# FFN chunks with stationary weights and two streaming token tiles in a one-core macaron layer

## The chip, the cores and the metric

The kernel runs on one core of a Trainium2 chip, in one launch. The metric is the device time of that launch in microseconds (us). The core has TensorE (PE; its weight loads are listed apart as PEld), VectorE (DVE), ScalarE (ACT), GpSimd (POOL), SyncE (SP, whose queue issues the weight transfers) and 16 DMA engines. PE multiplies a stationary operand of 128 x 128, which is loaded first, with a moving operand that streams through column by column, and adds into PSUM, here used as eight banks of 128 x 512 fp32.

## The reference

One decoder layer on 256 tokens of width 1024: an FFN, a token mixer, a second FFN, each behind an RMSNorm and a shift and scale that come from a vector c, and each added to h through a gate. The two FFNs are what the change touches:

```python
def swiglu(n, w_gate, w_up, w_down):
    return (jax.nn.silu(n @ w_gate) * (n @ w_up)) @ w_down
...
        sh1, sc1, gt1, sh2, sc2, gt2, sh3, sc3, gt3 = jnp.split(mod, N_MOD, axis=-1)
        n = modulate(rmsnorm(h, g_ffn1[l]), sh1, sc1)
        h = h + 0.5 * gt1 * swiglu(n, w1_gate[l], w1_up[l], w1_down[l])
        n = modulate(rmsnorm(h, g_mix[l]), sh2, sc2)
        h = h + gt2 * hybrid_mixer(n, w_in[l], w_pool[l], pool_scale[l], w_out[l])
        n = modulate(rmsnorm(h, g_ffn2[l]), sh3, sc3)
        h = h + 0.5 * gt3 * swiglu(n, w2_gate[l], w2_up[l], w2_down[l])
    return rmsnorm(h, g_final)
```

The shapes: n is 256 x 1024, w_gate and w_up are 1024 x 2816, w_down is 2816 x 1024, all fp32.

## The kernel before

**Numbers.** Every fp32 matrix is held as two parts, hi (rounded to the type fp32r, which PE takes) and lo (the rest, value minus hi). A product is three matmuls: hi by hi, lo by hi, hi by lo.

**Tiles.** The 256 tokens are two tiles of 128 (t = 0, 1). The width 1024 is eight k-tiles of 128. The 2816 hidden columns are 11 chunks of 256. All weights are read once, as transfers of 1 MB into one of four raw buffers, on SP's queue, in the order of the list that `plan` writes; each is then cast in two halves, hi on ACT (L290) and lo on DVE (L291), into 11 buffers of each kind. Units called "ada" in that list are not cast: DVE reduces them against c (L279) into the shifts, scales and gates, between the casts.

**Lead chunks and rest chunks.** The first chunks of each FFN (0 to 5 of FFN 1, 0 to 3 of FFN 2) are computed k-tile by k-tile while the normalised rows come in; the change leaves them as they are. The rest chunks are 6 to 10 of FFN 1 and 4 to 10 of FFN 2. For one of these, `ffn_chunk` (L399) computes for one token tile the 128 x 512 result "gate columns, then up columns" in one PSUM bank: tokens (128 x 128 of nh or nl) are stationary, and 512 weight columns stream, 8 k-tiles x 3 products = 24 matmuls (L396, L397). `swiglu` (L410) makes pr = Silu(gate) x up, tokens on the partitions: ACT's Silu reads PSUM (L413), DVE multiplies (L416). The second FFN product needs the hidden columns on the partitions, so `hidden_t` (L419) turns pr with two PE transposes per token tile (L422) and splits the turned tile into hh on ACT (L310) and hl on DVE (L311). `down` (L429) then multiplies these, stationary, with the down weights, 512 columns streaming, into accumulators (accf) that stand in four PSUM banks of their own (L437). Where the last two chunks of FFN 2 are added into half-banks, the matmuls are 256 columns wide (L449).

**Order.** `ffn_rest` (L494) runs over the rest chunks. In a turn it computes the chunk for t = 0, turns the chunk before it (L499), computes t = 1, and then runs down for the chunk before it. The last four chunks' down products (HOLD) are kept for the end of the FFN, where they lie under the residual's work. FFN 2's first rest chunk, 4, stands outside that loop (L909 to L913), and there it is the lead chunks 0 and 1 that are turned between the two token tiles. Small drains are marked urgent; the order of each engine's queue is set by a scheduler that goes by priorities and its own estimate of when things are ready. Pools decide which buffer a tile gets: `psp` has four PSUM banks, given out in turn, for chunk results, transposes and gates (`gate_rows`, one PE transpose behind chunk 9 of each FFN); a new tile in a bank waits until the last reader of the old one is done.

**Names in the trace.** gu is a chunk's result, ht a turned tile, le and ld lead chunks, prl their products, raw/hi/lo the weights, nha/nla the tokens of FFN 1 and nhc/nlc those of FFN 2; in a listing of instructions gu1_4_0 is FFN 2, chunk 4, token tile 0.

Of the kernel before, what the change touches and what calls it, by code (L numbers as in the profile page):

```python
# [10 lines left out]
F32 = mybir.dt.float32  # L11
# [161 lines left out]
def block_kernel(ctx, tc, w, vec, x, c, gf, wpool, bandd, biasd, out):  # L173
# [224 lines left out]

    def ffn_chunk(f, ci, n, t, between={}):  # L399
        ps = psp.tile([P, 512], F32, name=f"gu{f}_{ci}_{t}", tag="ps")  # L400
        for hf in range(2):
            hi, lo = want("gu", (f, ci, hf))
            for k in range(4):
                if 4 * hf + k in between:
                    between[4 * hf + k]()
                gemm(ps, n[t][0], n[t][1], 4 * hf + k, cols(hi, k), cols(lo, k),
                     hf == 0 and k == 0, hf == 1 and k == 3)
        return ps

    def swiglu(f, ci, t, ps, pr=None):  # L410
# [17 lines left out]

    def down(f, ci, t, hid, accs, banks=(0, 1)):  # L429
        hi, lo = want("down", (f, ci))  # L430
        hh, hl = hid
        steps = []
        for k in range(2):
            first, last = ci == 0 and k == 0, ci == NCH - 1 and k == 1
            for (a, ww, st, sp) in ((hh, hi, first, False), (hl, hi, False, False), (hh, lo, False, last)):
                for b in banks:
                    steps.append(mm(accs[b], a[:, k, :], cols(ww, 2 * k + b), start=st, stop=sp))  # L437
        return steps

    def down_halves(f, chunks, hid, acc_b, other):  # L440

        for c0, ps in ((0, acc_b), (256, other)):
            n = 0
            for ci in chunks:
                hi, lo = want("down", (f, ci))
                for k in range(2):
                    for a, ww in ((hid[ci][0], hi), (hid[ci][1], hi), (hid[ci][0], lo)):
                        n += 1
                        mm(ps[:, 0:256], a[:, k, :], cols(ww, 2 * k + 1)[:, c0:c0 + 256], start=c0 > 0 and n == 1,  # L449
                           stop=n == 6 * len(chunks))  # L450
# [42 lines left out]

    def ffn_rest(f, ci0, n, prev, pci, accs, finish, gate):  # L494
        hid = {}
        for ci in range(ci0, NCH):
            ps0 = ffn_chunk(f, ci, n, 0)
            pr0 = swiglu(f, ci, 0, ps0)
            hid[pci] = [hidden_t(f, pci, t, prev[t]) for t in range(NT)]  # L499
            ps1 = ffn_chunk(f, ci, n, 1)  # L500
            pr1 = swiglu(f, ci, 1, ps1)
            if pci < NCH - HOLD:
                for t in range(NT):
                    down(f, pci, t, hid[pci][t], accs[t])
            prev, pci = [pr0, pr1], ci
            if ci == NCH - 2:
                gate()
        last = range(NCH - HOLD, NCH)
        for ci in last[:-1]:
            down(f, ci, 0, hid[ci][0], accs[0])  # L510
        hid[NCH - 1] = [hidden_t(f, NCH - 1, t, prev[t]) for t in range(NT)]
        down(f, NCH - 1, 0, hid[NCH - 1][0], accs[0])
        after = finish(0)
        steps = []
        for banks in ((0, 1),) if f == 0 else ((0,), (1,)):
            for ci in last:
                if after and ci == last[TURN]:
                    after(steps)
                if f == 0 or banks == (0,) or ci < SPLIT[0]:
                    steps += down(f, ci, 1, hid[ci][1], accs[1], banks)  # L520
        if f == 1:
# [26 lines left out]
    xs, rs, turned = [], [], []  # L548
    n1 = [new_n(f"a{t}") for t in range(NT)]
    with in_order() as last:  # L550
# [81 lines left out]
    def hids(ci):  # L632
        return [hidden_t(0, ci, t, prs[ci][t]) for t in range(NT)]

    def both_down(ci, hid):
        for t in range(NT):
            down(0, ci, t, hid[t], nm["acc"][t])

# [102 lines left out]
    def heads_out(hp, v, y):  # L741
# [5 lines left out]
        with urgent():  # L747
            for t in range(NT):
                nc.scalar.copy(y[t][0][:, 4 + hp, :], ps[:, ts(t, P)])
            for t in range(NT):  # L750
                nc.vector.tensor_tensor(y[t][1][:, 4 + hp, :], ps[:, ts(t, P)], y[t][0][:, 4 + hp, :].bitcast(F32),
                                        ALU.subtract)

    def pool_group(g, u, y):
# [62 lines left out]
    def wout(t, banks, after=None):  # L817
        steps = []
        for n, i in enumerate(WOUT):
# [87 lines left out]

    prs = lead_out(1, lead, (2, 3, 0, 1))
    ps0 = ffn_chunk(1, LEAD, n3, 0)  # L909
    pr0 = swiglu(1, LEAD, 0, ps0)  # L910
    hid = [[hidden_t(1, ci, t, prs[ci][t]) for t in range(NT)] for ci in range(2)]
    ps1 = ffn_chunk(1, LEAD, n3, 1)
    pr1 = swiglu(1, LEAD, 1, ps1)  # L913
# [34 lines left out]
```

## Time and profile before

| | |
|---|---|
| median of 3 runs | 480.79 us (480.66 to 481.0) |
| the profiled execution | 481.04 us, of which the span (first to last instruction) is 479.2 us |
| granted PE clock, mean | 0.997 of full speed |
| FFN weights and others read | 124.61 MB, 262 GB/s over the span |
| FFN 1's rest chunks and downs | about 109.9 to 187 us |
| FFN 2's chunk 4, first rest chunk | starts near 330 us |

The rest of the page stands in the prediction, where it is used. In rows of groups the columns are line, engine, operation, out<-in, shapes and count, then busy us and mean ns of one, then the engine's idle time just before them and what ended it. In rows of a timeline they are start, duration, engine, line, operation; a row "x4" is four instructions in one.

### The profile page before, as it was taken

To read this page: it belongs to the slowest core of one execution; us is meant where nothing else is said; L and a number is where in the kernel's file an instruction comes from. 1 tells how busy PE (TensorE), PEld (TensorE's weight loads), DVE (VectorE), ACT (ScalarE), POOL (GpSimd) and SP (SyncE) were. 2 spreads that over 40 slices of the span, in tenths; PEclk is the share of its full clock that TensorE was granted. 3 is DMA by queue.
4 is the path that set the end of the run, shared out by engine and by line. 5 is a ranking of instruction groups with operands and counts; after the bars stand their busy time and mean duration, and the time that the engine had idled before them with its cause. 6 is when DMAs were issued, how large, how long until landed. Compare 5 with 4: busy or idle time off the path is not lost.

```text
span 479.2 us, 6028 instructions
## 1 busy us (share of the span) xinstructions
PE 469.0 (98%) x2188; PEld 381.2 (80%) x2188; DVE 355.8 (74%) x577; ACT 260.9 (54%) x447; POOL 13.4 (3%) x35
## 2 busy tenths in 40 slices
PE   8999999999999999999999999999999999999994
PEld 4678888888888888888878888888878888888883
DVE  4988899996987893789999868946666855655244
ACT  3686585454454460896877288845643543444121
POOL 1000000000000000110001000000000000000010
PEclk9999999999999999999999999999999999999998
DMA  8999995998988892579878944985457648630102
GB/s 302 412 349 345 358 347 186 351 420 356 351 316 329 302 379 122 221 279 377 334 284 334 346 177 178 376 324 176 176 180 271 260 191 327 230 122 0 44 1 88
DMA packets 19215, 126.05 MB, mean 263 GB/s; under 512 B 2329, under 2 KB 2865, under 8 KB 4850
## 3 DMA queue, kind: packets, MB, share of 16 engines
q1 hardware_dynamic: 17568, 121.12, 66.5%
q0 software_dynamic: 1184, 3.98, 2.4%
q10 hardware_dynamic: 434, 0.58, 0.3%
q8 instruction: 17, 0.28, 0.2%
q14 instruction: 12, 0.10, 0.1%
HBM read 124.61 MB, written 1.06 MB: 262 GB/s over the span
## 4 chain that ended last, share of the span: by engine, by line
PE 88%; ACT 5%; DMA 3%; issue 1%; DVE 1%; POOL 0%; POOLq 0%; DVEq 0%
PE accf L437 22%; PE gu L396 18%; PE gu L397 9%; PE le L485 9%; PE ld L485 8%; PE accm L829 5%; PE zp L396 4%; DMA raw<-in_w_dram 3%; PE zp L397 2%; PE ht L422 2%; ACT hi L290 2%; PE ld L396 2%; PE sh L396 2%; ACT nhb L367 1%; ACT n32b L368 1%
## 5 line engine op out<-in xcount | busy, mean ns | idle before, releaser
L291 DVE TENSOR_TENSOR lo<-raw,hi 128x1024 fp32r<-128x1024 f32 (+1 forms) x156 | 183.8, 1209 | 41.4 <-ACT hi L290 32.3
L290 ACT CAST hi<-raw 128x1024 fp32r<-128x1024 f32 (+1 forms) x156 | 158.2, 1045 | 74.9 <-DMA raw<-in_w_dram 32.3
L279 DVE CUSTOM_DVE_ANT_0 raw<-raw,cb,vecs 128x1024 f32<-128x1024 f32 x70 | 88.0, 1281 | 2.0 <-DMA raw<-in_w_dram 2.0
L437 PE MATMUL accf<-hi,hh 128*128 128x512 f32 x172 | 54.5, 394 | 0.2
L437 PE MATMUL accf<-hi,hl 128*128 128x512 f32 x172 | 54.2, 391 | 0.0
L437 PE MATMUL accf<-lo,hh 128*128 128x512 f32 x172 | 53.8, 389 | 0.0
L396 PE MATMUL gu<-hi,nhc 128*128 128x512 f32 x112 | 44.4, 396 | 0.0
L413 ACT ACTIVATE sg<-gu 128x256 f32<-128x256 f32 x24 | 9.2, 381 | 64.5 <-PE gu L397 64.5
L397 PE MATMUL gu<-lo,nhc 128*128 128x512 f32 x112 | 43.7, 390 | 0.0
L396 PE MATMUL gu<-hi,nlc 128*128 128x512 f32 x112 | 43.6, 390 | 0.0
L437 PEld LDWEIGHTS accf<-lo,hh 128*128 128x128 f32 x172 | 32.3, 188 | 6.8
L437 PEld LDWEIGHTS accf<-hi,hl 128*128 128x128 f32 x172 | 32.0, 188 | 7.2 <-DVE hl L311 0.7
L437 PEld LDWEIGHTS accf<-hi,hh 128*128 128x128 f32 x172 | 31.7, 188 | 7.2 <-ACT hh L310 1.1
L416 DVE TENSOR_TENSOR pr<-sg,gu 128x256 f32<-128x256 f32 x24 | 10.1, 419 | 33.1 <-ACT sg L413 33.1
L396 PE MATMUL gu<-hi,nha 128*128 128x512 f32 x80 | 31.7, 396 | 0.0
L397 PE MATMUL gu<-lo,nha 128*128 128x512 f32 x80 | 31.2, 390 | 0.0
L396 PE MATMUL gu<-hi,nla 128*128 128x512 f32 x80 | 31.1, 389 | 0.0
L311 DVE TENSOR_TENSOR hl<-ht,hh 128x256 fp32r<-128x256 f32 x44 | 16.5, 418 | 14.4 <-ACT hh L310 14.4
L310 ACT CAST hh<-ht 128x256 fp32r<-128x256 f32 x44 | 14.1, 379 | 23.0 <-PE ht L422 23.0
L396 PE MATMUL zp<-hi,nhb 128*128 128x512 f32 x64 | 26.1, 408 | 0.0
L397 PE MATMUL zp<-lo,nhb 128*128 128x512 f32 x64 | 25.0, 391 | 0.0
L396 PE MATMUL zp<-hi,nlb 128*128 128x512 f32 x64 | 25.0, 390 | 0.0
(193 smaller groups left out, 722.0 us busy)
## 6 DMA issues: line engine op xcount, KB each, us to landing
raw<-in_w_dram SPq DMA_DIRECT2D x112, 1024.0 KB, 5.7
raw<-in_w_dram SPq DMA_DIRECT2D x4, 512.0 KB, 7.8
gt<-gd POOLq DMA_DIRECT2D x3, 512.0 KB, 4.2
h<-in_x_dram SPq DMA_DIRECT2D x2, 512.0 KB, 4.7
bias<-in_bias_dram POOLq DMA_DIRECT2D x2, 512.0 KB, 3.7
band_all<-in_band_dram POOLq DMA_DIRECT2D x1, 544.0 KB, 3.6
gfb<-in_gf_dram POOLq DMA_DIRECT2D x1, 512.0 KB, 5.5
out_dram<-o SPq DMA_DIRECT2D x4, 128.0 KB, 2.5
```

Of the source, the lines that this page charges most:

```text
L279: note(nc.vector.tensor_tensor_reduce(r, r, cb, 1.0, vecs[:, m:m + 1], ALU.mult, ALU.add, mod[:, m:m + 1]), i, 1)
L290: note(nc.scalar.copy(hi[:, o:o + n], src), i + s / 2, 0)
L291: note(nc.vector.tensor_tensor(lo[:, o:o + n], src, hi[:, o:o + n].bitcast(F32), ALU.subtract), i + s / 2, 0)
L310: nc.scalar.copy(hi_ap, src)
L311: nc.vector.tensor_tensor(lo_ap, src, hi_ap.bitcast(F32), ALU.subtract)
L396: return [mm(ps, nh[:, k, :], whi, start=first, stop=False), mm(ps, nl[:, k, :], whi, start=False, stop=False), mm(ps, nh[:, k, :], wlo, s ...
L397: mm(ps, nh[:, k, :], wlo, start=False, stop=last)]
L416: nc.vector.tensor_tensor(pr, sg, ps[:, 256:512], ALU.mult)
L422: nc.tensor.transpose(pt[:, i, :], pr[:, ts(i, P)], ident)
L437: steps.append(mm(accs[b], a[:, k, :], cols(ww, 2 * k + b), start=st, stop=sp))
L485: done.append(mm(banks[ci][t], n[t][a][:, j, :], cols(ww, lead_set(f, j).index(ci)), start=j == 0 and p == 0, stop=last and p == 2))
L829: steps.append(mm(acc2[t][b], a[:, k, :], cols(ww, 2 * kk + b), start=st, stop=sp))
```

## The change

For the rest chunks the two operands change places. `block` computes 128 hidden columns (block b = 0 or 1 of the chunk's 256) for all 256 tokens: the weights are stationary, 128 x 128 at a time, and the tokens stream. The result has hidden columns on the partitions, so it needs no turning. A block fills two PSUM banks, e = 0 for gate and e = 1 for up. For each k-tile and each e there are two matmuls: the hi weights against hi and lo tokens of both tiles, 512 columns wide (hi results in the bank's first 256 columns, lo results in its last 256), and the lo weights against the hi tokens, 256 wide, added to the first 256 columns. When a block is done, ACT copies the last 256 columns of each bank out and DVE adds the first 256 to them; then follow Silu (ACT), the product (DVE) and the split into hh and hl (ACT, DVE), all on 128 x 256.

So that both tiles, hi and lo, can stream from one access, the token tiles lie in one SBUF tile `rounded` (as much memory as before; `homes` says which slot a new token tile takes). An operand of 512 columns is then four stretches of 128 in that tile. For the mixer's output y, tile 1 keeps its k-tiles in the order k ^ 4 (`slot`), the same work in other places. In the weight array, a rest chunk's two units are now cut by block b (all k-tiles of 128 gate and 128 up columns) and not by k-half; sizes and order of the transfers stay. In both FFNs the lead chunks that were turned inside a rest chunk are now turned between its block 0 and its block 1, once in FFN 1 (chunk 3's two token tiles, in chunk 6) and once in FFN 2 (those of chunks 0 and 1, in chunk 4).

The core of the diff:

```diff
+TURNED = (6, 4)
...
+        elif kind == "gu" and a[1] >= TURNED[a[0]]:
+            w[i].reshape(P, KD, 2, P)[:] = gu[a[0]][:, :, a[1], :, P * a[2]:P * a[2] + P].transpose(1, 0, 2, 3)
...
+    rounded = npool.tile([P, 2, 3, KD, P], F32R, name="rounded")
+    homes = iter((0, 1, 2, 1, 2, 0, 0, 1))
+
+    def new_n():
+
+        i = next(homes)
+        return rounded[:, 0, i], rounded[:, 1, i]
...
-    def ffn_chunk(f, ci, n, t, between={}):
-        ps = psp.tile([P, 512], F32, name=f"gu{f}_{ci}_{t}", tag="ps")
-        for hf in range(2):
-            hi, lo = want("gu", (f, ci, hf))
-            for k in range(4):
...
-                gemm(ps, n[t][0], n[t][1], 4 * hf + k, cols(hi, k), cols(lo, k),
-                     hf == 0 and k == 0, hf == 1 and k == 3)
...
+    def block(f, ci, b):
+
+        his, los = want("gu", (f, ci, b))
+        ps = [psp.tile([P, 2 * S], F32, name=f"bl{f}_{ci}_{b}{e}", tag="ps") for e in range(2)]
+        for k in range(KD):
+            for e in range(2):
+                o = slice((k % 4) * 2 * P + e * P, (k % 4) * 2 * P + e * P + P)
+                mm(ps[e].rearrange("p (a t c) -> p a t c", a=2, t=NT), his[k // 4][:, o], rounded[:, :, 0:NT, k, :],
+                   start=k == 0, stop=False)
+                mm(ps[e][:, 0:S].rearrange("p (t c) -> p t c", t=NT), los[k // 4][:, o], rounded[:, 0, 0:NT, k, :],
+                   start=False, stop=k == KD - 1)
...
+        with urgent():
...
+            for dst, src in ((sg, ps[0]), (pr, ps[1])):
+                nc.scalar.copy(dst, src[:, S:2 * S])
+                nc.vector.tensor_tensor(dst, src[:, 0:S], dst, ALU.add)
+            nc.scalar.activation(sg, sg, AF.Silu)
+            nc.vector.tensor_tensor(pr, pr, sg, ALU.mult)
+            split(hh, hl, pr)
+        return hh, hl
+
+    def blocks(f, ci, between={}):
+        both = []
+        for b in range(2):
+            both.append(block(f, ci, b))
+            if b in between:
+                between[b]()
+        return [[[a[:, ts(t, P)] for a in both[k]] for k in range(2)] for t in range(NT)]
...
         for ci in range(ci0, NCH):
-            ps0 = ffn_chunk(f, ci, n, 0)
-            pr0 = swiglu(f, ci, 0, ps0)
-            hid[pci] = [hidden_t(f, pci, t, prev[t]) for t in range(NT)]
-            ps1 = ffn_chunk(f, ci, n, 1)
-            pr1 = swiglu(f, ci, 1, ps1)
+            hid[ci] = blocks(f, ci, {0: turn_prev} if turn_prev else {})
+            turn_prev = None
             if pci < NCH - HOLD:
...
+    hid[LEAD] = blocks(1, LEAD, {0: lambda: hid.update({ci: hidden(1, ci, prs[ci]) for ci in range(2)})})
```

`down` and `down_halves` take their stationary slices from the new layout; they run the same matmuls.

**The order on the engines** at FFN 2's chunk 4. First PE of the kernel before, from the last matmul of token tile 0 to the first of tile 1 (ident is the unit matrix of a transpose, accf100 an accumulator; a number at a name's end only tells tiles apart):

```order
L397 MATMUL gu1_4_0_3097<-lo86_1_2911,nhc0_2683 128x512
L422 MATMUL ht1_0_0_3146<-ident_92,prl11_3072 128x128 x2
L422 MATMUL ht1_0_1_3153<-ident_92,prl11_3072 128x128 x2
L422 MATMUL ht1_1_0_3160<-ident_92,prl11_3072 128x128 x2
L437 MATMUL accf100_3203<-hi87_0_2947,hh1_0_0_3149 128x512
L437 MATMUL accf101_3204<-hi87_0_2947,hh1_0_0_3149 128x512
L422 MATMUL ht1_1_1_3167<-ident_92,prl11_3072 128x128 x2
L396 MATMUL gu1_4_1_3174<-hi85_0_2832,nhc1_2806 128x512
```

The same place on PE after the change, from the end of block 0 to the start of block 1:

```order
L437 MATMUL bl1_4_01_3193<-rounded_113,hi85_1_2921 128x512
L439 MATMUL bl1_4_01_3193<-rounded_113,lo85_1_2922 128x256
L418 MATMUL ht1_0_0_3238<-ident_92,prl11_3157 128x128 x2
L418 MATMUL ht1_0_1_3245<-ident_92,prl11_3157 128x128 x2
L418 MATMUL ht1_1_0_3252<-ident_92,prl11_3157 128x128 x2
L418 MATMUL ht1_1_1_3259<-ident_92,prl11_3157 128x128 x2
L470 MATMUL accf100_3322<-hi87_0_3032,hh1_0_0_3241 128x512
L470 MATMUL accf101_3323<-hi87_0_3032,hh1_0_0_3241 128x512
L470 MATMUL accf110_3324<-hi87_0_3032,hh1_0_1_3248 128x512
L437 MATMUL bl1_4_10_3276<-rounded_113,hi86_0_2991 128x512
```

The eight transposes and the first products of lead chunks 0 and 1 stand between the two halves of chunk 4 in both; the last two transposes moved ahead of those products, and a third product came in. Now ACT at that place, first before, then after:

```order
L413 ACTIVATE sg1_4_0_3142<-gu1_4_0_3097 128x256
L310 CAST hh1_0_0_3149<-ht1_0_0_3146 128x256
L310 CAST hh1_0_1_3156<-ht1_0_1_3153 128x256
L310 CAST hh1_1_0_3163<-ht1_1_0_3160 128x256
L310 CAST hh1_1_1_3170<-ht1_1_1_3167 128x256
```

```order
L447 COPY sg1_4_0_3228<-bl1_4_00_3192 128x256
L293 CAST hi91_0_3268<-raw91_3266 128x1024
L447 COPY pr1_4_0_3229<-bl1_4_01_3193 128x256
L449 ACTIVATE sg1_4_0_3228<-sg1_4_0_3228 128x256
L313 CAST hh1_4_0_3226<-pr1_4_0_3229 128x256
L313 CAST hh1_0_0_3241<-ht1_0_0_3238 128x256
```

Where Silu stood alone ahead of the casts of the turned tiles, there are now two copies with a weight cast (hi91_0) between them, Silu and the cast of block 0. DVE there, after the change:

```order
L448 TENSOR_TENSOR sg1_4_0_3228<-bl1_4_00_3192,sg1_4_0_3228 128x256
L294 TENSOR_TENSOR lo91_0_3269<-raw91_3266,hi91_0_3268 128x1024
L448 TENSOR_TENSOR pr1_4_0_3229<-bl1_4_01_3193,pr1_4_0_3229 128x256
L450 TENSOR_TENSOR pr1_4_0_3229<-pr1_4_0_3229,sg1_4_0_3228 128x256
L314 TENSOR_TENSOR hl1_4_0_3227<-pr1_4_0_3229,hh1_4_0_3226 128x256
L314 TENSOR_TENSOR hl1_0_0_3242<-ht1_0_0_3238,hh1_0_0_3241 128x256
```

The weight cast lo91_0 stands between the two adds; before, the multiplication of gu1_4_0 stood there, followed at once by the four subtractions of the turned tiles. In FFN 1 the second half of chunk 7 on DVE reads, before and after:

```order
L416 TENSOR_TENSOR pr0_7_1_1305<-sg0_7_1_1303,gu0_7_1_1278 128x256
L291 TENSOR_TENSOR lo41_1_1223<-raw41_1216,hi41_1_1222 128x1024
L291 TENSOR_TENSOR lo42_0_1241<-raw42_1238,hi42_0_1240 128x1024
L291 TENSOR_TENSOR lo42_1_1245<-raw42_1238,hi42_1_1244 128x1024
L279 ISA raw43_1307,mod_100<-raw43_1307,cb_91,vecs_95 128x1024
```

```order
L448 TENSOR_TENSOR sg0_7_1_1348<-bl0_7_10_1312,sg0_7_1_1348 128x256
L448 TENSOR_TENSOR pr0_7_1_1349<-bl0_7_11_1313,pr0_7_1_1349 128x256
L294 TENSOR_TENSOR lo41_1_1253<-raw41_1246,hi41_1_1252 128x1024
L450 TENSOR_TENSOR pr0_7_1_1349<-pr0_7_1_1349,sg0_7_1_1348 128x256
L294 TENSOR_TENSOR lo42_0_1305<-raw42_1302,hi42_0_1304 128x1024
L314 TENSOR_TENSOR hl0_7_1_1347<-pr0_7_1_1349,hh0_7_1_1346 128x256
L294 TENSOR_TENSOR lo42_1_1309<-raw42_1302,hi42_1_1308 128x1024
```

The steps of a drain moved in between the casts and reductions of weights.

More of the change, by code (lines that the diff above doesn't have):

```diff
@@ L427, in hidden_t, with hidden, down @@
         return hh, hl
-    def down(f, ci, t, hid, accs, banks=(0, 1)):
+    def hidden(f, ci, prs):
+        tiles = [hidden_t(f, ci, t, prs[t]) for t in range(NT)]
+        return [[[a[:, k, :] for a in tiles[t]] for k in range(2)] for t in range(NT)]
+    def block(f, ci, b):
[8 more added lines that the diff above has]
+                   start=False, stop=k == KD - 1)
+        hh = fp[0].tile([P, S], F32R, name=f"hh{f}_{ci}_{b}", tag="hh", bufs=8)
+        hl = fp[0].tile([P, S], F32R, name=f"hl{f}_{ci}_{b}", tag="hl", bufs=8)
+        with urgent():
+            sg = fp[0].tile([P, S], F32, name=f"sg{f}_{ci}_{b}", tag="sg", bufs=2)
+            pr = fp[0].tile([P, S], F32, name=f"pr{f}_{ci}_{b}", tag="pr", bufs=4)
+            for dst, src in ((sg, ps[0]), (pr, ps[1])):
[12 more added lines that the diff above has]
+        return [[[a[:, ts(t, P)] for a in both[k]] for k in range(2)] for t in range(NT)]
+    def down(f, ci, rows, accs, banks=(0, 1)):
         hi, lo = want("down", (f, ci))
-        hh, hl = hid
         steps = []
         for k in range(2):
+            hh, hl = rows[k]
             first, last = ci == 0 and k == 0, ci == NCH - 1 and k == 1
@@ L436, in down, with down_halves @@
                 for b in banks:
-                    steps.append(mm(accs[b], a[:, k, :], cols(ww, 2 * k + b), start=st, stop=sp))
+                    steps.append(mm(accs[b], a, cols(ww, 2 * k + b), start=st, stop=sp))
         return steps
-    def down_halves(f, chunks, hid, acc_b, other):
+    def down_halves(f, chunks, rows, acc_b, other):
         for c0, ps in ((0, acc_b), (256, other)):
@@ L446, in down_halves @@
                 for k in range(2):
-                    for a, ww in ((hid[ci][0], hi), (hid[ci][1], hi), (hid[ci][0], lo)):
+                    hh, hl = rows[ci][k]
+                    for a, ww in ((hh, hi), (hl, hi), (hh, lo)):
                         n += 1
-                        mm(ps[:, 0:256], a[:, k, :], cols(ww, 2 * k + 1)[:, c0:c0 + 256], start=c0 > 0 and n == 1,
+                        mm(ps[:, 0:256], a, cols(ww, 2 * k + 1)[:, c0:c0 + 256], start=c0 > 0 and n == 1,
                            stop=n == 6 * len(chunks))
@@ L492, in lead_out, with ffn_rest @@
                 for i, ci in enumerate(chunks)}
[L494 to L495 removed]
+    def ffn_rest(f, ci0, hid, pci, accs, finish, gate, turn_prev=None):
         for ci in range(ci0, NCH):
[L497 to L501 removed]
+            hid[ci] = blocks(f, ci, {0: turn_prev} if turn_prev else {})
+            turn_prev = None
             if pci < NCH - HOLD:
                 for t in range(NT):
[L504 to L505 removed]
+                    down(f, pci, hid[pci][t], accs[t])
+            pci = ci
             if ci == NCH - 2:
@@ L509, in ffn_rest @@
         for ci in last[:-1]:
-            down(f, ci, 0, hid[ci][0], accs[0])
-        hid[NCH - 1] = [hidden_t(f, NCH - 1, t, prev[t]) for t in range(NT)]
-        down(f, NCH - 1, 0, hid[NCH - 1][0], accs[0])
+            down(f, ci, hid[ci][0], accs[0])
+        down(f, NCH - 1, hid[NCH - 1][0], accs[0])
         after = finish(0)
@@ L519, in ffn_rest @@
                 if f == 0 or banks == (0,) or ci < SPLIT[0]:
-                    steps += down(f, ci, 1, hid[ci][1], accs[1], banks)
+                    steps += down(f, ci, hid[ci][1], accs[1], banks)
         if f == 1:
@@ L548, in block_kernel @@
     xs, rs, turned = [], [], []
-    n1 = [new_n(f"a{t}") for t in range(NT)]
+    n1 = [new_n() for t in range(NT)]
     with in_order() as last:
@@ L632, in hids @@
     def hids(ci):
-        return [hidden_t(0, ci, t, prs[ci][t]) for t in range(NT)]
+        return hidden(0, ci, prs[ci])
     def both_down(ci, hid):
         for t in range(NT):
-            down(0, ci, t, hid[t], nm["acc"][t])
+            down(0, ci, hid[t], nm["acc"][t])
     def finish1(t):
@@ L748, in heads_out @@
             for t in range(NT):
-                nc.scalar.copy(y[t][0][:, 4 + hp, :], ps[:, ts(t, P)])
+                nc.scalar.copy(y[t][0][:, slot(t, 4 + hp), :], ps[:, ts(t, P)])
             for t in range(NT):
-                nc.vector.tensor_tensor(y[t][1][:, 4 + hp, :], ps[:, ts(t, P)], y[t][0][:, 4 + hp, :].bitcast(F32),
-                                        ALU.subtract)
+                nc.vector.tensor_tensor(y[t][1][:, slot(t, 4 + hp), :], ps[:, ts(t, P)],
+                                        y[t][0][:, slot(t, 4 + hp), :].bitcast(F32), ALU.subtract)
     def pool_group(g, u, y):
@@ L767, in pool_group @@
             for t in range(NT):
-                nc.scalar.activation(y[t][0][:, g, :], p2[:, ts(t, P)], AF.Copy, scale=sc)
+                nc.scalar.activation(y[t][0][:, slot(t, g), :], p2[:, ts(t, P)], AF.Copy, scale=sc)
             for t in range(NT):
-                nc.vector.scalar_tensor_tensor(y[t][1][:, g, :], p2[:, ts(t, P)], sc, y[t][0][:, g, :].bitcast(F32),
-                                               ALU.mult, ALU.subtract)
+                nc.vector.scalar_tensor_tensor(y[t][1][:, slot(t, g), :], p2[:, ts(t, P)], sc,
+                                               y[t][0][:, slot(t, g), :].bitcast(F32), ALU.mult, ALU.subtract)
     after = finish1(1)
@@ L778, in block_kernel, with slot @@
     QS = -DH ** -0.5
-    y = [new_n(f"y{t}") for t in range(NT)]
+    y = [new_n() for t in range(NT)]
+    def slot(t, k):
+        return k ^ 4 if t else k
     z = {}
@@ L828, in wout @@
                     for b in banks:
-                        steps.append(mm(acc2[t][b], a[:, k, :], cols(ww, 2 * kk + b), start=st, stop=sp))
+                        steps.append(mm(acc2[t][b], a[:, slot(t, k), :], cols(ww, 2 * kk + b), start=st, stop=sp))
     n3 = {}
@@ L908, in block_kernel @@
     prs = lead_out(1, lead, (2, 3, 0, 1))
[L909 to L913, printed above, removed]
+    hid = {}
+    hid[LEAD] = blocks(1, LEAD, {0: lambda: hid.update({ci: hidden(1, ci, prs[ci]) for ci in range(2)})})
     nm["acc"] = new_acc("f1")
@@ L916, in block_kernel @@
         if ci > 1:
-            hid.append([hidden_t(1, ci, t, prs[ci][t]) for t in range(NT)])
+            hid[ci] = hidden(1, ci, prs[ci])
         for t in range(NT):
-            down(1, ci, t, hid[ci][t], nm["acc"][t])
-    ffn_rest(1, LEAD + 1, n3, [pr0, pr1], LEAD, nm["acc"], finish3, lambda: nm.update(g3=gate_rows(GT3, 0.5)))
+            down(1, ci, hid[ci][t], nm["acc"][t])
+    ffn_rest(1, LEAD + 1, hid, LEAD, nm["acc"], finish3, lambda: nm.update(g3=gate_rows(GT3, 0.5)))
     finish3(1)
```

13 lines of the change are left out of this document (4 added, 9 removed).

## The prediction

> **What bounds the kernel now.** I read the share of each engine first, then the chain of work that ended last, then a table of one stretch.
>
> ```profile
> span 479.2 us, 6028 instructions
> PE 469.0 (98%) x2188; PEld 381.2 (80%) x2188; DVE 355.8 (74%) x577; ACT 260.9 (54%) x447; POOL 13.4 (3%) x35
> PE 88%; ACT 5%; DMA 3%; issue 1%; DVE 1%; POOL 0%; POOLq 0%; DVEq 0%
> ```
>
> PE is busy 98% of the span and makes 88% of the chain, so the time is PE's time: what an instruction on PE takes less is won, and what DVE and ACT do is free until PE has to wait for it. The stretch where the other engines have least room is FFN 1's rest chunks. Columns below: stretch, then busy time and count of PE, PEld, DVE, ACT, POOL, granted clock, DMA share, GB/s.
>
> ```profile
> 109.90:176.90 67.00, 67.00 (x308) 55.33 (x307) 54.91 (x75) 32.18 (x48) 1.29 (x2) 1.00 0.86 331
> ```
>
> PE has no gap in these 67.00 us, DVE is idle for 67.00 − 54.91 = 12.09 us, ACT for 35, and the DMA engines are 86% busy.
>
> **The matmuls.** A matmul's "busy" time covers its pipeline, so its price is the distance between starts.
>
> ```profile
> 340.00 0.39 PE L397 MATMUL gu<-lo,nhc 128*128 128x512 f32 x1
> ...
> 342.04 0.39 PE L397 MATMUL gu<-lo,nhc 128*128 128x512 f32 x1
> 469.32 0.28 PE L449 MATMUL accf<-hi,hh 128*128 128x256 f32 x1
> ...
> 472.07 0.28 PE L449 MATMUL far<-lo,hh 128*128 128x256 f32 x1
> ```
>
> The first pair are the 1st and 10th of ten 512-wide matmuls in a row: 2.04 / 9 = 0.2267 us each. The second pair are the 1st and 24th of 24 that are 256 wide: 2.75 / 23 = 0.1196 us. The 256 columns between them cost 0.1071 us, so either shape is its columns plus about 0.0125 us. A chunk had 2 × 24 × 0.2267 = 10.88 us; now it has 32 of 512 columns and 32 of 256, 32 × (0.2267 + 0.1196) = 11.08 us. Twelve chunks are changed (6 to 10 of FFN 1, 4 to 10 of FFN 2): 12 × 0.20 = **+2.4 us**.
>
> More weight loads run, 64 for 48 in a chunk.
>
> ```profile
> L437 PEld LDWEIGHTS accf<-hi,hh 128*128 128x128 f32 x172 | 31.7, 188 | 7.2 <-ACT hh L310 1.1
> L449 PEld LDWEIGHTS far<-hi,hh 128*128 128x128 f32 x4 | 0.8, 192 | 0.0
> ```
>
> They cost nothing here: a 0.188-us load already fits each 0.2267-us step, and the 256-wide matmuls keep their 0.1196 us with a 0.192-us load each, so loads lie under the matmuls ahead of them.
>
> [...]
>
> **The turns that go.** A chunk's four transposes, and the clearing of PE around them, stand in PE's own row.
>
> ```profile
> L422 PE MATMUL ht<-ident,pr 128*128 128x128 f32 x48 | 7.2, 272 | 0.0
> 457.43 0.62 PE L437 MATMUL accf<-lo,hh 128*128 128x512 f32 x2
> 457.88 0.60 PE L422 MATMUL ht<-ident,pr 128*128 128x128 f32 x4
> 458.24 0.48 PE L437 MATMUL accf<-hi,hh 128*128 128x512 f32 x1
> 458.56 0.39 PE L437 MATMUL accf<-hi,hl 128*128 128x512 f32 x1
> 458.78 0.68 PE L437 MATMUL accf<-hi,hh 128*128 128x512 f32 x2
> ```
>
> The 48 are gone. Without the four at 457.88, the three 512-wide matmuls after them would have started at 457.88, 458.11 and 458.33; the last did at 458.78, that is 0.45 us late, from the first matmul of the group to the last one shown. I take 0.44 a group: 12 × 0.44 = **−5.3 us**.
>
> **Entry of FFN 2, chunk 4.** The eight transposes of leads 0 and 1 stay, and now stand between block 0 and block 1 of that chunk.
>
> ```profile
> 334.85 0.39 PE L397 MATMUL gu<-lo,nhc 128*128 128x512 f32 x1
> 335.08 0.82 PE L422 MATMUL ht<-ident,prl 128*128 128x128 f32 x6
> 335.98 0.73 PE L437 MATMUL accf<-hi,hh 128*128 128x512 f32 x2
> 336.54 0.38 PE L422 MATMUL ht<-ident,prl 128*128 128x128 f32 x2
> 336.68 0.48 PE L396 MATMUL gu<-hi,nhc 128*128 128x512 f32 x1
> 335.28 0.39 ACT L413 ACTIVATE sg<-gu 128x256 f32<-128x256 f32 x1 [2.22 <-PE gu L397]
> 335.56 0.92 ACT L310 CAST hh<-ht 128x256 fp32r<-128x256 f32 x3
> L290 ACT CAST hi<-raw 128x1024 fp32r<-128x1024 f32 x152 | 155.9, 1056 | 71.9 <-DMA raw<-in_w_dram 29.4 <-PE accf L437 21.3 <-PE gu L396 11.4
> L291 DVE TENSOR_TENSOR lo<-raw,hi 128x1024 fp32r<-128x1024 f32 x152 | 181.2, 1223 | 41.0 <-ACT hi L290 31.8 <-PE le L485 6.6
> ```
>
> Before, 335.08 to 336.68 is 1.60 us for 8 × 0.11 + 2 × 0.227 = 1.33 us of work: a loss of 0.27 us. Now block 0 holds two of the four PSUM banks instead of one, and the third and fourth transposed tiles (ht1_1_0, ht1_1_1) need them back. The first is free when DVE's add into sg1_4_0 ends, the second when the add into pr1_4_0 ends. That second add stands, in the order of the engines, behind ACT's weight cast hi91_0, ACT's copy and DVE's lo91_0. With T the first transpose: copy sg to T + 0.23; its add to T + 0.69; hi91_0 (1.056) to T + 1.18; lo91_0 (1.223) to T + 2.43; copy pr (0.38) to T + 1.46; add pr (0.42, starting in the writes of lo91_0) to T + 2.77. So ht1_1_1 turns at T + 2.8 instead of T + 0.66. Queued behind it on PE are three matmuls of leads 0 and 1, which wait for hh1_0_0; this ACT cast stands behind the mult (T + 3.1) and hh1_4_0 (T + 3.5), so it ends at T + 3.8, and block 1 starts at T + 3.8 + 3 × 0.227 = T + 4.5. Unstalled it would be T + 0.88 + 0.68 = T + 1.56. The stall is 2.9 us, less the 0.27 lost before: **+2.65 us**. Its ends are 0 (hi91_0 and lo91_0 long done, as where their weights came early) and 3.3 (the whole chain, with a further 0.4-us operation); I take the walk, since these two casts come from a transfer of the same chunk.
>
> **Entry of FFN 1, chunk 6.** The same with four transposes. Only two banks are taken by them, but block 1 needs block 0's back: its first matmul waits for an add that ends at about T + 0.73, with 0.44 us of transposes to cover it: **+0.3 us**; from 0 to 1.4, should a 1.056-us cast stand ahead of the copy. The two gate transposes behind chunk 9 wait for an add too, under three matmuls: +0.1 in all.
>
> **What must hide.** Each block adds two ACT copies and two DVE adds, and the drain becomes copy, add, Silu, mult, cast, subtract.
>
> ```profile
> L413 ACT ACTIVATE sg<-gu 128x256 f32<-128x256 f32 x24 | 9.2, 381 | 64.5 <-PE gu L397 64.5
> L310 ACT CAST hh<-ht 128x256 fp32r<-128x256 f32 x44 | 14.1, 379 | 23.0 <-PE ht L422 23.0
> L416 DVE TENSOR_TENSOR pr<-sg,gu 128x256 f32<-128x256 f32 x24 | 10.1, 419 | 33.1 <-ACT sg L413 33.1
> 132.61 0.42 DVE L416 TENSOR_TENSOR pr<-sg,gu 128x256 f32<-128x256 f32 x1 [1.76 <-ACT sg L413]
> 132.94 0.75 DVE L311 TENSOR_TENSOR hl<-ht,hh 128x256 fp32r<-128x256 f32 x2
> ```
>
> The step from one such DVE operation to the next is 0.33 us (132.61 to 132.94). In FFN 1's stretch, 4.5 chunks × 4 adds × 0.335 = 6.0 us stand against 12.1 us of idle DVE, most of it waits for PE as at 132.61. A block's two banks are wanted again one block (16 × 0.346 = 5.5 us) later. I cost this at nothing; without that cover it is the second rival. The end of each FFN is covered: 36 downs (8.2 us) lie between the last block and the use of its rows, against a drain of some 3 us (two copies, two adds, Silu, mult, cast, subtract at 0.38 to 0.42).
>
> **Sum.** 481.04 (the profiled execution) − 5.3 + 2.4 + 2.65 + 0.3 + 0.1 = 481.2; the rounding of the two large terms goes either way by 0.2. The median of the runs is 0.25 lower than this execution, the lowest run 0.4; I give **481.1 us**: no change that can be told, the bound being 0.2% (0.96 us), about what a measurement of this kernel can tell.
>
> **Rivals.**
> - *The entry does not stall* (0.20). If hi91_0 and lo91_0 stand elsewhere in time (ahead of the block's end, while ACT is idle: 2.22 us before 335.28), both adds end by T + 1.1, inside the transposes. For it: ACT and DVE have waits there. Against: the order puts both casts between the copies. 481.1 − 2.65 = 478.4, down to 478.0 without FFN 1's 0.3.
> - *DVE cannot keep up in FFN 1* (0.17), the slower side. Each block makes DVE turn to ACT three times (two copies, Silu). If nothing stands between, that is 10 blocks × 3 × 0.38 = 11.4 us, with the adds 17.4 against 12.1 idle: 5.3 us late at FFN 1's end. Raw buffers then come free late, and transfers (DMA 86% busy) cannot catch up. It decides once DVE is later than the last block's slack, 8.2 − 3 = 5.2 us, or the 5.5 us of a bank. Between 0 and 5.3 I take 3: 484.1. Against it: the order has casts between the turns.
> - *Streaming in four runs of 128 columns costs a start each* (0.05). No row of before streams such an operand. At 0.0125 us for each further run, a chunk has 32 × 3 + 32 × 1 = 128, so 12 × 128 × 0.0125 = 19 us: 500. The change would then not do what it says.
> - *The further loads are exposed* (0.01), if loads of one kind of weights could not slip under the other's matmuls: 12 × 16 × 0.188 = 36 us, 517. The row with 0.192-us loads at 0.1196-us steps speaks against it.
> - *The clock falls in the entry's stall* (0.03). The row of the stretch shows 1.00, and nothing in FFN 2 stops PE long. If a stop of 2.9 us halved the clock for as long again, the work in that time would take 1.5 us more: 482.6.
>
> [...]
>
> **Chances.** The forecast, with either sign of its small terms (480.2 to 482.2), has 0.54: 0.42 within 0.2%, 0.10 slower, 0.02 faster. With the rivals: faster 0.02 + 0.20 = 0.22; same 0.42; slower 0.10 + 0.17 + 0.05 + 0.01 + 0.03 = 0.36. The range takes in the unstalled entry (478.0) and the late DVE up to 484.3; it leaves out the exposed runs and loads and the worse half of the late DVE, some 0.15.
>
> **What would show it.** Right: no transposes in the rest chunks; starts in a block 0.227 and 0.120 us apart; one gap of some 2.9 us in PE at FFN 2's chunk 4, released by DVE's add and ACT's hh; PE gapless in FFN 1 but for 0.3 us. Wrong: pairs in a block further apart than 0.346 us, gaps at the starts of blocks 7 to 10, a PE clock below 1.00 behind the entry, or a chunk 4 without a gap.

## The result, and the profile after

The changed kernel takes 485.0 us (median of 4 runs, 483.1 to 486.8) where the kernel before takes 480.8: a ratio of 1.0081, 95% interval 1.0059 to 1.0102. It is slower, by 4 us, and its runs lie 3.7 us apart where those of before, measured with them, lie within 0.4. The profiled execution is the slowest of the four, 486.82 us.

The page of the changed kernel: span, engines, clock in 40 slices, chain.

```profile
span 485.0 us, 6414 instructions
PE 473.2 (98%) x2332; PEld 390.1 (80%) x2332; DVE 373.1 (77%) x625; ACT 275.7 (57%) x495; POOL 14.5 (3%) x35
PEclk9999999999999999999999999999799999999998
PE 95%; DVE 1%; DMA 1%; ACT 1%; issue 0%; POOL 0%; POOLq 0%; DVEq 0%
```

PE still bounds the kernel, and more of the chain is its own. What is new is one 7 in the clock, in the slice from 339 us on. DVE carries 17 us more and ACT 15 us, and neither shows in FFN 1, in the stretch that the prediction looked at (columns as there, from a table of stretches of the changed kernel):

```profile
109.90:176.90 67.00, 66.87 (x365) 57.20 (x364) 58.82 (x93) 37.83 (x66) 1.29 (x2) 1.00 0.83 317
```

PE is idle for 0.13 us of these 67, though DVE is now busy for 58.8 of them. The place of the 7 is FFN 2's chunk 4. Its timeline on PE, DVE and ACT (start, duration, engine, line, operation, idle time before it):

```profile
335.85 0.28 PE L439 MATMUL bl<-rounded,lo 128*128 128x256 f32 x1
335.97 1.17 PE L418 MATMUL ht<-ident,prl 128*128 128x128 f32 x6
338.78 0.60 PE L418 MATMUL ht<-ident,prl 128*128 128x128 f32 x2 [1.64 <-DVE pr L448]
340.01 1.65 PE L470 MATMUL accf<-hi,hh 128*128 128x512 f32 x3 [0.63 <-ACT hh L313]
341.46 0.63 PE L437 MATMUL bl<-rounded,hi 128*128 128x512 f32 x1
341.89 0.41 PE L439 MATMUL bl<-rounded,lo 128*128 128x256 f32 x1
336.22 0.42 DVE L448 TENSOR_TENSOR sg<-bl,sg 128x256 f32<-128x256 f32 x1 [0.34 <-ACT sg L447]
337.16 1.23 DVE L294 TENSOR_TENSOR lo<-raw,hi 128x1024 fp32r<-128x1024 f32 x1 [0.52 <-PE ht L418]
338.30 0.42 DVE L448 TENSOR_TENSOR pr<-bl,pr 128x256 f32<-128x256 f32 x1
335.81 0.37 ACT L447 COPY sg<-bl 128x256 f32<-128x256 f32 x1 [1.24 <-PE bl L439]
336.08 1.05 ACT L293 CAST hi<-raw 128x1024 fp32r<-128x1024 f32 x1
337.03 0.38 ACT L447 COPY pr<-bl 128x256 f32<-128x256 f32 x1
```

With T = 335.97 the walk of the prediction can be read off: the weight cast stands between the two copies, its subtraction between the two adds, and the last transposes run at T + 2.81 (forecast T + 2.8), the first product at T + 4.04 (forecast 3.8). But from there every step is nearly twice as long as ahead of the stall: 341.46 to 341.89 is 0.43 us for a 512-wide matmul, where the one at 335.61 took 0.24 to the next start, 335.85. The granted clock in a table of four stretches, ahead of, in and behind it:

```profile
335.50:338.80 3.30, 1.52 (x11) 1.00 (x9) 2.37 (x5) 1.91 (x4) 0.00 (x0) 1.00 0.53 204
338.80:342.20 3.40, 2.77 (x8) 1.99 (x9) 2.18 (x6) 1.50 (x5) 0.00 (x0) 0.52 0.26 111
342.20:345.70 3.50, 3.50 (x12) 2.95 (x12) 0.00 (x0) 0.00 (x0) 0.00 (x0) 0.50 0.00 0
345.70:349.00 3.30, 3.30 (x21) 2.89 (x20) 1.23 (x1) 1.15 (x2) 0.00 (x0) 0.99 0.00 0
```

PE is granted half its clock for 6.8 us behind the stall. About 1.1 us of that PE waited anyway, so by the granted clock 5.7 us of work took double: an estimate of 2.9 us lost.

The second difference is small and everywhere. The first two rows of the timeline below are the starts of blocks 0 and 1 of FFN 2's chunk 9, the third the start of its last block, the fourth what follows that one:

```profile
433.30 0.40 PE L437 MATMUL bl<-rounded,hi 128*128 128x512 f32 x1
438.96 0.40 PE L437 MATMUL bl<-rounded,hi 128*128 128x512 f32 x1
450.49 0.40 PE L437 MATMUL bl<-rounded,hi 128*128 128x512 f32 x1
456.04 0.40 PE L470 MATMUL accf<-hi,hh 128*128 128x512 f32 x1
```

A block is 16 pairs of a 512-wide and a 256-wide matmul. The first takes 5.66 us, 0.354 a pair, the last 5.55 us, 0.347. The forecast was 0.3463 (0.2267 + 0.1196). Twenty of the 24 blocks run at 0.353 or 0.354. So a whole rest chunk with its 24 downs gains nothing. The same span of work before and after, from the start of FFN 2's chunk 6 to that of chunk 7, first in the timeline of the kernel before:

```profile
381.89 0.39 PE L396 MATMUL gu<-hi,nhc 128*128 128x512 f32 x1
398.70 0.39 PE L396 MATMUL gu<-hi,nhc 128*128 128x512 f32 x1
```

and in that of the changed kernel:

```profile
388.43 0.39 PE L437 MATMUL bl<-rounded,hi 128*128 128x512 f32 x1
405.22 0.39 PE L437 MATMUL bl<-rounded,hi 128*128 128x512 f32 x1
```

16.81 us with the turns, 16.79 us without them.

The profiled execution is 5.8 us longer in its span than that of before. By stages (first matmul to first matmul): FFN 1's rest chunks +0.1, FFN 2's rest chunks +5.1, the start and FFN 1's leads +0.9, the other stages −0.4. The 0.9 lies in the first 15 us, ahead of the chunks that were changed, and four of the seven profiles below have under 0.15 us of it.

### The profile page after: what moved, and what is told of

Its sections match the earlier page's. It is cut to its first block, busy times and chain, and to the rows that moved or that the text cites. A ratio compares the mean times of both kernels' runs of the same rounds, so it can differ in the third digit from the quotient of the medians.

```text
span 485.0 us, 6414 instructions
## 1 busy us (share of the span) xinstructions
PE 473.2 (98%) x2332; PEld 390.1 (80%) x2332; DVE 373.1 (77%) x625; ACT 275.7 (57%) x495; POOL 14.5 (3%) x35
## 4 chain that ended last, share of the span: by engine, by line
PE 95%; DVE 1%; DMA 1%; ACT 1%; issue 0%; POOL 0%; POOLq 0%; DVEq 0%
PE accf L470 24%; PE bl L437 19%; PE bl L439 9%; PE ld L519 9%; PE le L519 9%; PE zp L403 6%; PE accm L864 5%; PE zp L404 3%; PE ld L403 2%; PE sh L403 2%; DMA h<-in_x_dram 1%; PE ld L404 1%; PE sh L404 1%; PE yt L776 1%; PE sc L737 1%; PE xt L321 1%
## 5 line engine op out<-in xcount | busy, mean ns | idle before, releaser
L437 PE MATMUL bl<-rounded,hi 128*128 128x512 f32 x384 | 138.0, 403 | 0.1
L439 PE MATMUL bl<-rounded,lo 128*128 128x256 f32 x384 | 108.0, 282 | 0.0
L437 PEld LDWEIGHTS bl<-rounded,hi 128*128 128x128 f32 x384 | 73.1, 190 | 18.6 <-DVE sg L448 0.6
L439 PEld LDWEIGHTS bl<-rounded,lo 128*128 128x128 f32 x384 | 73.5, 191 | 0.6
L403 PE MATMUL zp<-hi,rounded 128*128 128x512 f32 x128 | 40.7, 399 | 0.0
L519 PE MATMUL ld<-hi,rounded 128*128 128x512 f32 x128 | 33.5, 399 | 0.0
L519 PE MATMUL le<-hi,rounded 128*128 128x512 f32 x128 | 32.4, 390 | 0.0
L519 PEld LDWEIGHTS ld<-hi,rounded 128*128 128x128 f32 x128 | 24.3, 192 | 6.0 <-DVE rounded L500 0.8
L519 PEld LDWEIGHTS le<-hi,rounded 128*128 128x128 f32 x128 | 24.0, 188 | 4.9
L404 PE MATMUL zp<-lo,rounded 128*128 128x512 f32 x64 | 25.0, 391 | 0.0
```

Source lines behind the costliest of these rows:

```text
L403: return [mm(ps, nh[:, k, :], whi, start=first, stop=False), mm(ps, nl[:, k, :], whi, start=False, stop=False), mm(ps, nh[:, k, :], wlo, s ...
L404: mm(ps, nh[:, k, :], wlo, start=False, stop=last)]
L437: mm(ps[e].rearrange("p (a t c) -> p a t c", a=2, t=NT), his[k // 4][:, o], rounded[:, :, 0:NT, k, :], start=k == 0, stop=False)
L439: mm(ps[e][:, 0:S].rearrange("p (t c) -> p t c", t=NT), los[k // 4][:, o], rounded[:, 0, 0:NT, k, :], start=False, stop=k == KD - 1)
L519: done.append(mm(banks[ci][t], n[t][a][:, j, :], cols(ww, lead_set(f, j).index(ci)), start=j == 0 and p == 0, stop=last and p == 2))
```

## The experiments

The theory after the result has two parts. The **stall** at chunk 4 comes from the weight casts in block 0's drain, and PE's idleness there makes the clock fall, for a time that differs from one execution to the next. The **pair** of matmuls takes 0.007 us more than its parts did before.

**The changed kernel again**, with no edit.

> The changed kernel once more. Theory (the clock gate): the stall at FFN 2's chunk 4 is the same in every execution, about 2.9 us, and what differs is for how long the granted clock is halved behind it. Undisturbed the kernel would need about 483.3 us (forecast 481.2 plus 384 pairs of matmuls at 0.352 instead of 0.346 us, 2.1 us); each execution lies above that by half of the time at half clock, so its time follows its mean granted clock: near 483 at 0.996, near 487 at 0.990. Rival (transfers or another engine vary): times between 483 and 487 that do not follow the clock.

485.5 us (484.7 to 487.3), ratio 1.0099 (1.0078 to 1.0120). All eight executions of the changed kernel, time against mean granted clock: 483.1 at 0.996, 484.7 at 0.995, 485.1 at 0.993, 484.9, 485.5 and 485.6 at 0.992, 486.8 and 487.3 at 0.990. By and large they follow the clock. In the profiles of before and after the clock is also at half for the last 2.4 and 2.7 us, behind the last matmul, and the runs of the kernel before, whose profile has no other half clock, show means of 0.995 to 0.998. So, by their means, the six executions at 0.993 or less had a half clock at the entry; of those at 0.995 and 0.996 it cannot be said. In the profile of this run the stall is the same (two stops, released by the same two instructions):

```profile
338.44 0.44 PE L418 MATMUL ht<-ident,prl 128*128 128x128 f32 x2 [1.64 <-DVE pr L448]
339.68 1.60 PE L470 MATMUL accf<-hi,hh 128*128 128x512 f32 x3 [0.80 <-ACT hh L313]
```

but the half clock is shorter, in its table of stretches:

```profile
339.41:342.82 3.41, 3.14 (x9) 2.56 (x10) 1.73 (x5) 1.03 (x4) 0.00 (x0) 0.55 0.00 0
342.82:346.24 3.42, 3.42 (x21) 3.03 (x20) 0.26 (x1) 1.05 (x1) 0.00 (x0) 0.95 0.00 0
```

In the first 3.41 us 45% of the full clock is missing, in the next 3.42 us 5%, together 1.7 us; at half clock that is 3.4 us, half of the 6.8 above.

**The stall filled with work.** 16 and 7 idle matmuls on PE where it waits.

```diff
+        fill = spin_between(16) if (f, ci, t) == (1, 1, 1) else []
         for i in range(2):
-            nc.tensor.transpose(pt[:, i, :], pr[:, ts(i, P)], ident)
+            one = nc.tensor.transpose(pt[:, i, :], pr[:, ts(i, P)], ident)
...
+        if (f, ci, t) == (1, 1, 1):
+            nm["fill"] = spin_between(7)[-1]
```

> 16 idle matmuls (the unit matrix, bf16, 256 wide, into an accumulator bank that is cleared afterwards) are put on PE between the transposes of ht1_1_0 and ht1_1_1, and 7 between those of ht1_1_1 and the first product of lead chunk 0: PE is busy while it would wait, and nothing else moves. Theory (the clock falls because PE idles there): the stall stays, block 1 still starts about 4.5 to 4.8 us after the first transpose, the clock stays at 1.00, and the time is 483.3 with a spread under 0.5 us. Rival (the clock falls for another reason, the four-stretch operand or the load on the chip): half clock behind the stall as before and 484 to 487.

483.9 us (483.4 to 485.4), ratio 1.0069 (1.0050 to 1.0089). In its profile, the entry in the timeline, and the stretch behind it in the table of stretches:

```profile
335.24 1.17 PE L420 MATMUL ht<-ident,prl 128*128 128x128 f32 x6
336.25 1.91 PE L440 MATMUL accf<-ident 128*128 128x256 bf16 x16
338.06 0.44 PE L420 MATMUL ht<-ident,prl 128*128 128x128 f32 x2
338.33 0.93 PE L440 MATMUL accf<-ident 128*128 128x256 bf16 x7
339.30 0.96 PE L484 MATMUL accf<-hi,hh 128*128 128x512 f32 x3
340.10 0.40 PE L451 MATMUL bl<-rounded,hi 128*128 128x512 f32 x1
```

```profile
339.41:342.82 3.41, 3.41 (x19) 2.93 (x20) 1.35 (x5) 0.66 (x3) 0.00 (x0) 1.00 0.00 0
```

The wait is as long (the last transposes at T + 2.8), the clock stays at 1.00, and block 1 starts at T + 4.86. The kernel does more work and is 1.6 us faster than the unfilled one measured with it. So here it is PE's idleness that lowers the clock, and that is worth 1.6 us in the median and, by the estimate above, 2.9 in the execution of 486.82 us. The spread was not under 0.5 us: one of the four took 485.4, and why is not shown; the kernel before, too, has a single execution 2 us above its median (483.0).

In the profile of 486.82 us PE's two stops were 1.64 and 0.63 us by the releasers, and the clock fell at 338.92, behind the first of them alone.

**The weight casts behind the turned tiles.** The stall without the casts in the drain.

```diff
+    want("gu", (1, LEAD + 1, 0))
+    for s in range(2):
+        for e in range(2):
+            order_dep(casts[("gu", (1, LEAD + 1, 0)), s][e], nm["turned"][e].ins, "casts later")
```

> The four casts of one weight unit (hi91, lo91) are ordered behind the casts of the turned tiles, so that no weight cast stands between the copies and adds of block 0. Theory (those casts make the stall): the second add ends about 1.1 us after the first transpose T instead of 2.8; what is left is the chain copies, adds, Silu, mult, cast, cast (hh1_0_0 at about T+2.2), so block 1 starts at about T+2.9 instead of T+4.5: 1.6 us less, no half clock, 481.7. Rival (the bank's drain is slow by itself, or PE waits for hh1_0_0 alone): block 1 at T+4 or later, 483 to 486.

482.1 us (10 runs, 481.7 to 483.1), ratio 1.0020 (1.0011 to 1.0030).

```profile
335.40 1.52 PE L419 MATMUL ht<-ident,prl 128*128 128x128 f32 x8
337.75 0.96 PE L471 MATMUL accf<-hi,hh 128*128 128x512 f32 x3 [0.83 <-ACT hh L314]
338.55 0.40 PE L438 MATMUL bl<-rounded,hi 128*128 128x512 f32 x1
```

All eight transposes run in one piece, the first product starts at T + 2.35 and block 1 at T + 3.15 (forecast 2.9), and the clock stays at 1.00. One order of four casts is worth 3.4 us: 1.7 of stall (4.86 − 3.15, from the filled kernel) and the clock. The casts are about half of the stall: block 1 at T + 3.15 is still 1.6 us behind the T + 1.56 that the prediction gives for an entry without a stall, and those are the drain's own steps up to hh1_0_0.

The half clock has two lengths. In the first profile of the changed kernel the clock falls at 338.92 and stays at half for 6.83 us; in its second it falls at 339.76 and stays at half for 3.41 us. Stretches of 3.4 us, as long as the shorter of the two, first the one that ends where the clock falls in the first profile, then the same in the second, then one that holds the stop of the present kernel:

```profile
335.51:338.92 3.41, 1.63 (x11) 1.11 (x10) 2.45 (x6) 1.91 (x4) 0.00 (x0) 1.00 0.55 211
336.34:339.76 3.42, 0.96 (x5) 0.49 (x5) 2.36 (x5) 1.85 (x6) 0.00 (x0) 1.00 0.70 287
335.89:339.31 3.42, 2.45 (x13) 1.74 (x13) 2.72 (x8) 2.79 (x8) 0.00 (x0) 1.00 0.84 307
```

Behind the stretches with PE busy for 1.63 and 0.96 us the clock was halved, behind the one with 2.45 us it was not. In the first profile the 3.41 us behind the fall still held the second stop (PE busy for 2.78 us of them), and the clock stayed at half for 3.42 us more; in the second profile that stop was over at 339.68, ahead of the fall, PE was busy throughout the 3.41 us at half clock, and the full clock came back at their end. So in these two profiles the longer half clock is the one with a stop of PE in it. Whether the stop sets the length was not tested by a change.

**The turns inside block 1.** No stall at all.

```diff
         for k in range(KD):
+            if mid and k == 6:
+                mid()
             for e in range(2):
...
-    hid[LEAD] = blocks(1, LEAD, {0: lambda: hid.update({ci: hidden(1, ci, prs[ci]) for ci in range(2)})})
+    hid[LEAD] = blocks(1, LEAD, {1: lambda: hid.update({0: hidden(1, 0, prs[0])})})
...
-        if ci > 1:
+        if ci > 0:
             hid[ci] = hidden(1, ci, prs[ci])
```

> The turned tiles of lead chunk 0 are transposed inside block 1 of chunk 4 (at k-tile 6), those of lead chunk 1 behind it with the products, and in FFN 1 chunk 3's inside block 1 of chunk 6. Block 1 then needs nothing of block 0's drain, which has 4 us. Theory: no stop of PE over 0.5 us in FFN 2, clock at 1.00, 483.3 - 2.65 = 480.6. Rival (the wait only moves: the tiles of lead chunk 1 need the banks of block 1, whose drain has the same casts in it): a stop of 1 to 3 us behind block 1, 482 to 485.

480.6 us (10 runs, 480.0 to 481.2), ratio 0.9989 (0.9979 to 0.9998, just clear of 1), the expected time. In FFN 2 no two starts on PE stand further apart than 0.51 us, and those are two products. The wait did not move. With the stall gone, the change as such comes out 0.6 us ahead of the 481.2 measured with it: the turns' gain less the blocks' extra.

**Two stretches in place of four.** This and the next two stand on the kernel with the turns inside block 1.

```diff
-    rounded = npool.tile([P, 2, 3, KD, P], F32R, name="rounded")
+    rounded = npool.tile([P, 2, KD, 3, P], F32R, name="rounded")
```

> The kernel with the turns inside block 1 (480.6), with the token tiles laid out so that the 512-column operand is two stretches of 256 columns and not four of 128, and the 256-column one a single stretch. What is asked is why a pair of matmuls takes 0.353 us in most blocks and not 0.346. Theory (a state that PE falls into when a block begins: single blocks of the changed kernel, the last of FFN 2 and that behind the filled stall, kept 0.347 with the same four stretches): pairs still at 0.353 in most blocks, 480.6. Rival (each further stretch costs): pairs near 0.348, 384 x 0.005 = 1.9 us less, 478.7.

480.5 us (480.0 to 481.3), ratio 0.9986 (0.9973 to 0.9999): no difference from the 480.6 with four stretches. From the start of chunk 9's first block to that of its second:

```profile
426.60 0.40 PE L439 MATMUL bl<-rounded,hi 128*128 128x512 f32 x1
432.26 0.40 PE L439 MATMUL bl<-rounded,hi 128*128 128x512 f32 x1
```

The pairs stay at 0.354 us. Two stretches more in the operand cost nothing that shows, and one of the prediction's rivals falls.

**Both wide matmuls first.**

```diff
             for e in range(2):
                 o = slice((k % 4) * 2 * P + e * P, (k % 4) * 2 * P + e * P + P)
                 mm(ps[e].rearrange("p (a t c) -> p a t c", a=2, t=NT), his[k // 4][:, o], rounded[:, :, 0:NT, k, :],
                    start=k == 0, stop=False)
+            for e in range(2):
+                o = slice((k % 4) * 2 * P + e * P, (k % 4) * 2 * P + e * P + P)
                 mm(ps[e][:, 0:S].rearrange("p (t c) -> p t c", t=NT), los[k // 4][:, o], rounded[:, 0, 0:NT, k, :],
```

> The kernel with the turns inside block 1 (480.6), with the matmuls of a k-tile in the order 512 wide for gate, 512 for up, 256 for gate, 256 for up, instead of 512, 256, 512, 256. Theory (the alternation of a weight load under a short matmul with one under a long one sets the 0.353): the four take 0.693 us, the sum of twice 0.2267 and twice 0.1196, instead of 0.706: 192 x 0.013 = 2.5 us less, 478.1. Rival (stretches, or one state for any order): 0.706 for the four, 480.6.

478.5 us (478.2 to 478.9), ratio 0.9948 (0.9934 to 0.9963), faster than both kernels. The same block, 9's first, and the starts of chunks 6 and 7:

```profile
425.38 0.63 PE L439 MATMUL bl<-rounded,hi 128*128 128x512 f32 x2
430.95 0.62 PE L439 MATMUL bl<-rounded,hi 128*128 128x512 f32 x2
381.07 0.62 PE L439 MATMUL bl<-rounded,hi 128*128 128x512 f32 x2
397.65 0.62 PE L439 MATMUL bl<-rounded,hi 128*128 128x512 f32 x2
```

5.57 us a block, 0.348 a pair, and 16.58 us a chunk where it was 16.79 (forecast of the prediction: 16.81 − 0.44 + 0.20 = 16.57). Of the 0.21 us, 0.15 lie in the two blocks and 0.06 in the 24 downs behind them (5.44 us in place of 5.50 by the starts on PE in chunk 6). The order 512, 256, 512, 256 cost about 2 us in all (480.5 with it, measured together with these 478.5).

**Gate products ahead of up products.**

```diff
-        for k in range(KD):
-            for e in range(2):
+        for e in range(2):
+            for k in range(KD):
```

> The kernel with the turns inside block 1 (480.6), with a block's gate products all ahead of its up products: 16 matmuls into one bank, then 16 into the other, so the bank changes once in a block and not with every pair, and the gate bank is drained during the up products. Theory (the alternation of loads sets the pair's 0.353, whatever the bank): 0.353 a pair, 480.6, at most 0.3 less through the earlier drain. Rival (the change of bank costs 0.007 us a pair): 0.346 a pair, 2.5 us less, 478.1.

479.7 us (479.5 to 480.2), ratio 0.9975 (0.9965 to 0.9985). Its pairs stand at 0.353 us in 20 of 24 blocks and at 0.347 in the last two of each FFN. So the change of bank with each pair is not what costs: with one bank throughout, the alternation still runs at 0.353. One rival is left: the kernel with the wide matmuls first also never has two matmuls in a row into one bank, as both alternating kernels have, and no run holds the widths and changes that alone. Rows of one width run into one bank at the full pace, 0.2267 and 0.1196, so it would have to be a cost of mixed widths only. The 0.8 us gained on the kernel with two stretches, measured with this one, lie in the last two blocks of each FFN: they take 5.63 and 5.55 us in both FFNs, there 5.92 and 5.66. Of that 0.4 is their pace, the rest a shorter stop behind the gate's transpose.

## Why the prediction was wrong

Point by point, by its own steps:

- *The turns that go, −5.3 us*: right. A chunk at 16.58 us in the kernel with the wide matmuls first is 0.23 us shorter than before, with blocks 2 × 5.57 = 11.14 us long against 10.88; the turns were worth 0.23 + 0.26 = 0.49 us in a chunk, forecast 0.44. The reading stopped a row early: the next start on PE, 459.30, is 0.51 us late.
- *The blocks, +2.4 us*: mis-sized. The prediction added a 512-wide and a 256-wide step that it had measured each among its own kind, 0.3463 a pair. In alternation they took 0.353, so the term was 384 × 0.353 − 12 × 10.88 = +5.0 us, and the change's whole gain was gone. This is the first step that failed: that steps measured in rows of one width, each with its weight load, add up in a mixed order. The rows of before have no such order, and the prediction gave it no rival of its own. Its rival for a slower stream named the operand's stretches, which is refuted.
- *Entry of FFN 2, +2.65 us*: mechanism, place, releasers and length right. By the gaps in the rows the last transposes came at T + 2.81, the first product at T + 4.04; at full clock block 1 would follow at T + 4.7, forecast 4.5.
- *The clock falls in the stall*: this was a rival with a chance of 0.03 and 1.5 us, and the sum has it at nothing. It shows in at least six of eight executions and costs 1.6 us in the median. This is the second step that failed: that a stop of 2.9 us, in two pieces, would leave the clock at 1.00. The trace of before has no such stop ahead of its last matmul; in the profile of 486.82 us the clock fell behind the first piece alone, 1.64 us.
- *Entry of FFN 1, +0.3*: right to the hundredth. In the rows of the changed kernel block 1 begins 0.73 us after the first of four transposes.

```profile
116.33 0.60 PE L418 MATMUL ht<-ident,part 128*128 128x128 f32 x4
117.06 0.50 PE L437 MATMUL bl<-rounded,hi 128*128 128x512 f32 x1
```

- *The gates behind chunk 9, +0.1 in all*: too small. The block behind each gate's transpose takes 0.2 to 0.3 us longer than the others, some 0.5 us in both FFNs. In the rows of the changed kernel the block in FFN 1 lasts 5.92 us, from the first start to the second:

```profile
167.61 0.47 PE L437 MATMUL bl<-rounded,hi 128*128 128x512 f32 x1
173.53 0.40 PE L437 MATMUL bl<-rounded,hi 128*128 128x512 f32 x1
```

- *What must hide*: right. The rival that DVE cannot keep up (484.1) came close to the measured time by another road; PE was never short of FFN 1's casts.

The sum with the three terms corrected: 481.1 + 2.6 (pairs) + 0.2 (stall) + 1.6 (clock) = 485.5; measured 485.0 and 485.5. The smaller differences, −0.6 for the turns, +0.4 for the gates and about +0.4 for the downs behind alternating blocks, nearly cancel, so the agreement to a tenth is luck. Two of the signs that the prediction named for being wrong came: pairs further apart than 0.346 us, and a clock below 1.00 behind the entry.

What stays open: why the alternating order costs, and why single blocks run it at 0.347. They are blocks that PE enters behind a stop or a filled wait, or that follow a block with such a stop in it (a gate's transpose), and not all such blocks do it. So the order is shown to matter, and the mechanism is not.

## What to carry to other kernels

Here a stall of PE cost its length and then the clock behind it: 3.1 us (T + 4.7 at full clock in place of T + 1.56) were followed by 3.4 or 6.8 us at half clock, which cost another 1.6 us in the median and 2.9 by the estimate for the longer one, so price such a stall at up to twice its length, or put other work into it; with the casts behind the turned tiles a stop of 0.83 us left the clock at 1.00. Step times measured in rows of one width (0.2267 + 0.1196 = 0.346) did not add up for the mixed sequence (0.353 a pair); here it paid, by about 2 us, to put matmuls of one width in twos. Where a drain has several steps, look at which unrelated long instruction the order puts between them: here a weight cast between two copies and its subtraction between two adds were worth 3.4 us.

## What the runs showed of the hardware that was not expected

- PE's clock fell to half behind a stop of 1.64 us (behind two of 1.64 and 0.80 us in the second profile), came back after 3.4 or 6.8 us, and idle matmuls in the gap kept it at 1.00. Stretches of 3.4 us with PE busy for 1.63 and 0.96 us were followed by half clock, one with 2.45 us was not.
- 512-wide and 256-wide matmuls with a new weight load each take 0.353 us a pair in alternation (0.347 in a few blocks), 0.348 in twos, where rows of one width give 0.2267 + 0.1196 = 0.346.
- A moving operand of four stretches of 128 columns streams as fast as one of two stretches of 256: 0.354 us a pair in both, 480.6 and 480.5 us.
